# Hybrid decoder step on one core: another listed order of the instructions on all five engines

## Chip, cores and metric

The kernel runs on one core of a Trainium2 chip. The metric is device time in microseconds. The engines are PE (TensorE; PEld is its weight loads), DVE (VectorE), ACT (ScalarE), POOL (GpSimd) and SP (SyncE, which issues the transfers here). Each engine works through its own instructions strictly in the order in which they stand, and waits where an instruction needs something that another engine or a transfer has not delivered.

## What is computed

One step of a one-layer decoder, for a prompt of 2048 tokens and 8 samples of 8 new tokens each, model width 1024, all in f32:

```python
h = rmsnorm(x, norm_w)
z = h @ w_in
q, k, v, qb, kb, vb, g_lr, gate_a, gate_b = jnp.split(z, split_points(), axis=-1)
...
q = rope(rmsnorm(heads(q, H_A), q_norm_w), pos)
k = rope(rmsnorm(heads(k, H_A), k_norm_w), pos)
o_a = attend(q, k, v)
log_a = jax.nn.log_sigmoid((g_lr @ w_gate_up + b_gate).astype(jnp.float32)) / GATE_TAU
o_b, s_fin = gla_chunked(heads(qb, H_B) * (DK_B ** -0.5), heads(kb, H_B), heads(vb, H_B),
                         heads(log_a, H_B), s0)
o_b = rmsnorm(o_b, gla_norm_w)
mixed = jnp.concatenate([o_a.reshape(B, L, D_A) * jax.nn.silu(gate_a.astype(jnp.float32)),
                         o_b.reshape(B, L, D_B) * jax.nn.silu(gate_b.astype(jnp.float32))], axis=-1)
y = x + mixed.astype(x.dtype) @ w_out
```

`attend` mixes three dilated windows, (128,1), (512,4) and (2048,16), over 8 heads of 64. For the samples it reads a cache of 2048 keys and values. `gla_chunked` is gated linear attention, 4 heads with keys of 64 and values of 128. The outputs are y, the new keys and values and the final states.

## The kernel before

**Stages.** Weights and activations are split into a high and a low f16 part, so a projection of 128 rows by 512 columns is 24 matmuls of 128x128 weights on 512 columns (8 blocks of depth, 3 products): `project`, line 1632, tiles `acc_v`, `acc_q`, `acc_k`, `acc_qkb`, `acc_g`, `acc_vb`, `acc_gb`. The stages overlap:

- up to about 30 us: rows of x are scaled, turned and split (`prep_first`), and the weights w_v are scaled;
- to about 400 us: the v, q and k projections, and from 148 us on among them the window attention (`attend`): scores `s` (line 902), exp `p` on DVE and ACT (910, 913), transposes `t` (920), their split `pt` (877 to 887) and products `O` (935);
- to about 740 us: the rest of that attention, the last dilated branch from 534 us on, beside the qkb, g and vb projections (574 to 819 us for g and vb) with their silu (`so_g`, lines 1171 to 1185, on DVE and ACT);
- to about 1070 us: gated linear attention (`gla_core`, `gla_prompt`), first the samples', from 819 us on beside the gb projection, from 981 us on beside the output projection `Y` (`finish`, line 1991);
- to the end: `Y`, the turning of its inputs (`tm`, line 1956), and the samples' attention (`sample_pair`).

**Narrow matmuls.** Most matmuls use all 128x128 of TensorE's array. Some name a smaller part of it, a tile of the array. Their output then fills only some partitions, for instance 64 or 32, and others may fill the rest:

- `sc_e` (line 746, scores of gated linear attention): 128x64 tiles on 64 columns of f32, eight to a level, in turn for partitions 0 to 63 and 64 to 127;
- `U` (line 1790, the state's update): 128x64 tiles on 128 columns, four to a chunk of 128 tokens, two for each half;
- `R` (line 2182, the samples' scores) and `OS` (line 2248, their values): 128x32 tiles, in fours, one for each quarter of the partitions;
- `O_s` (1857), `U_s` (1890), `u_e` (681), `ptg_smp` (669) and the lower halves of the samples' projections (line 1323), fewer of each.

In the source the four OS of a step stand together:

```python
                for x, (u, bb) in enumerate(QUADS):
                    PE.matmul(
                        OS[32 * x : 32 * x + 32, 0:256], ps(x),
                        vs_[bb][:, 256 * u : 256 * u + 256],
                        start=(i == 0), stop=(i == 13),
                    )
```

**ScalarE's tables.** The first statement, `ACT.preload_act_table_set("natural_log_exp_and_others")` at line 566, loads the one set of tables that serves ln, exp, square and copy alike. Where ACT meets a function that the loaded set lacks, the build puts a load ahead of it.

**What sets the order.** The source is written in an order made by generators that `weave` takes turns with. That order is not the one that runs: at the end `in_order` (line 546) reads, for each engine, a list of numbers from `ORDER`, the places of the engine's instructions as written, and chains the instructions in the listed order:

```python
    for e, runs in ORDER.items():
        ends = [[int(n) for n in r.split("-")] for r in runs.split()]
        order = [traced[e][n] for r in ends for n in range(r[0], r[-1] + 1)]
        assert len(order) == len(traced[e])
        for a, b in zip(order, order[1:]):
            tc.add_manual_dep(b, a.name, info, reason="listed order")
```

The waits between engines follow from the data and the buffers, whatever the list. 8019 numbers stand for PE, 2014 for DVE, 1731 for ACT, 474 for POOL and 1055 for SP.

Of the kernel before, what the change touches and what calls it, by code (L numbers as in the profile page):

```python
# [53 lines left out]
        "6-8 0 2-3 1 10 4-5 9 11-25 74 90-91 75 92-93 76-77 94-99 78-79 100-111 80-89 112-113 26-33 42-46 "  # L54
        "34-41 47-65 116-129 140-146 66 147-160 67-68 161 114 69-71 162 72-73 163 130-131 115 132-139 "
        "164-212 214-218 213 219-281 286 282-283 287 284 288 285 289-295 310-312 296-298 313 299-304 314 "
        "305-309 315-387 390-392 397 426 398-399 427 404-405 428 406 433 409 434 410 435 411 440 416 441 "
        "417 442 418 447 421 448-449 422 454-455 423 456 461-463 468-470 475-477 484-486 491-493 500-502 "
        "509-511 516-518 525-527 532-534 539 546-548 557-559 564-566 571 540 572-573 541 582-584 587-589 "
        "592-594 601-603 610-612 615-617 622-624 629-634 639-641 658 646 659 647 660 665-667 670-671 648 "  # L60
        "672 651 675 652 676-677 653 682-684 689-691 694 706-708 711 695 712-713 696 716 699 717 700 718 "
        "701 723-725 730-732 735-737 742 754-756 761-763 743 766 744 767 749 768 750 771 751 772-773 "
        "778-780 785-787 792-794 799-801 806-808 811-813 818-820 827-829 836-838 843-845 852-854 861-863 "
        "866-868 873-875 884-886 891-893 898-900 388-389 393-396 400-401 909-911 916-918 407-408 412 402 "
        "413 419 403 420 424 414 425 415 921-923 930-931 429 932 939-941 944-945 443-446 946 436-439 430 "
        "457-458 431-432 464-465 459-460 466-467 450-453 489-490 494-495 471 953-955 962 514-515 519-520 "
        "963 482-483 487-488 507-508 512-513 472-474 478-481 496-499 503-506 521 964 967 542-545 968-969 "
        "567-570 972-973 535-538 560-563 522-524 528-531 549 974 574 979-980 984 550-555 575-581 597 556 "
        "590-591 595-596 985-986 613-614 618 991 598-600 604-607 585-586 992 608 993 609 619 998-999 620 "
        "1000 1003 635-638 1004 654-657 1005 981 621 625-626 642 627 643 628 644-645 649-650 1010-1012 "  # L70
        "661 1015-1017 662-664 680 1022 673-674 678-679 681 685-686 1023 668 692-693 669 697-698 1024 687 "
        "1027 688 1028-1029 702 1034-1036 703-705 714-715 721 719-720 709 1037 733-734 738-739 722 "
        "726-727 1038 710 1039 728 1040 729 752-753 757 740 758 774-777 1041 741 745-748 1042-1043 759 "
        "1044-1045 769 1046-1047 760 764-765 770 1048-1049 1056-1057 781 795-798 1058 816-817 788 782-784 "
        "802 789 821 790-791 1059 822 1060 809-810 1061 814-815 1062 823 1063-1067 803-805 824-826 "
        "830-833 1068-1071 841-842 846 834-835 847 869-870 848 871-872 839-840 859 849-851 855-856 860 "
        "876 857-858 864-865 887 877-883 888 894-897 901 889-890 919-920 924-925 902-908 926 912-915 "
        "927-928 937 942-943 947-948 929 933-936 965-966 970-971 938 960 949 961 950-952 975 956-958 "
        "1078-1080 1083 987-988 976-977 989-990 1084-1085 1006-1009 959 982 1086-1087 983 1088 1093-1095 "
        "1100-1101 1025-1026 1030-1031 1102 1105-1107 1124-1126 1131-1132 1112 1133 1054-1055 1113 1138 "  # L80
        "1114 1139 1119 1140 1120 1145 1121 1146-1147 1152-1154 1161-1163 1170-1172 1175-1177 1001 "
        "1182-1184 1193-1195 1200-1201 1072-1073 1202 1207-1209 1218-1219 1248-1250 1255 1220 1256 978 "
        "994 1225 995-997 1257 1226 1264 1227 1265 1230 1266 1231 1273 1232 1274 1239 1275 1240-1241 "
        "1280-1282 1285-1287 1296-1297 1310-1312 1321 1298 1322 1303 1323 1304 1328 1305 1329-1330 1002 "
        "1335-1337 1342-1344 1351 1013-1014 1018-1019 1352 1032 1353 1020 1052-1053 1358 1376-1378 "
        "1383-1385 1359 1392 1033 1050-1051 1360 1021 1393 1367 1394 1368 1399 1369 1400-1401 1089-1091 "
        "1406 1108-1110 1081 1074 1092 1111 1082 1075-1077 1407 1096-1098 1438 1408 1099 1439 1413 "
        "1103-1104 1440 1414 1449 1415 1450 1424 1122 1451 1425 1454 1426 1143-1144 1148-1149 1455 1431 "
        "1123 1129 1150 1127 1456 1432 1130 1151 1128 1115-1117 1134 1155 1118 1433 1461 1135 1157 1156 "
        "1462 1136-1137 1141-1142 1463 1466 1158-1160 1164-1167 1185 1467-1468 1477 1502-1503 1186 1504 "  # L90
        "1187 1478 1188 1509 1479 1510 1189-1190 1168 1196-1197 1191 1198 1192 1199 1169 1484 1178 1203 "
        "1173 1511 1179 1204 1174 1485 1180 1205 1181 1514 1206 1486 1515 1491 1516 1492 1523 1493 "
        "1524-1525 1532 1210 1533-1534 1539 1228 1253 1540 1221 1246-1247 1211 1251 1212-1213 1252 "
        "1214-1217 1235-1236 1222 1237-1238 1223 1242-1243 1229 1254 1224 1233 1258 1541 1564 1234 1259 "
        "1565 1548 1244 1566 1245 1549 1569 1550 1570 1557 1571 1558 1260 1580 1559 1581 1271 1261-1262 "
        "1272 1263 1267 1278 1299-1300 1306 1268-1269 1276 1279 1307 1277 1283 1301 1270 1288 1302 1582 "
        "1289-1290 1308 1291-1292 1284 1293 1309 1294 1587 1295 1588 1626 1589 1627 1594 1628 1595 1635 "
        "1596 1636 1605 1637 1606 1642 1324 1349-1350 1354-1355 1607 1313 1643 1314-1315 1325 1316 1612 "
        "1317 1326 1644 1318-1319 1327 1613 1320 1338 1651 1339-1340 1614 1341 1331 1356 1345 1652 1346 "
        "1332 1357 1347 1619 1348 1333 1361 1620 1653 1660 1621 1334 1362 1661-1662 1667 1363-1366 1668 "  # L100
        "1370-1373 1669 1388-1391 1381 1676 1374-1375 1409 1395 1379 1396 1382 1410 1380 1402-1403 "
        "1397-1398 1386 1411 1404-1405 1677 1387 1412 1678 1683-1685 1416 1690-1691 1417-1418 1692 "
        "1419-1420 1697-1699 1708-1709 1427-1430 1421-1423 1710 1452-1453 1434 1459-1460 1464 1457-1458 "
        "1441 1435-1437 1465 1442-1448 1715 1754-1756 1763 1487-1488 1764-1765 1770 1469-1472 1771 "
        "1473-1475 1489 1476 1772 1480-1481 1494 1490 1512-1513 1482 1517-1518 1483 1505 1495-1496 1506 "
        "1779 1497-1498 1507 1499-1500 1508 1716 1780 1501 1717 1781 1722 1788 1519 1723 1789 1520-1521 "
        "1724 1522 1790 1793-1795 1800 1530-1531 1733-1734 1555 1535 1556 1735 1560-1561 1738 1526-1528 "
        "1536 1529 1739 1801 1537 1740 1802 1562 1538 1563 1542 1745 1543 1572 1811 1567-1568 1544-1545 "
        "1746 1812 1546-1547 1551 1747 1552 1573-1579 1597-1602 1813 1553-1554 1603-1604 1590-1592 "
        "1583-1584 1615-1616 1585-1586 1617 1593 1618 1818-1820 1825-1827 1608-1609 1640 1610 1641 "  # L110
        "1645-1646 1611 1622 1665-1666 1670-1671 1836-1838 1623-1625 1629-1631 1633-1634 1632 1843-1844 "
        "1647 1845 1638-1639 1848-1849 1878 1658-1659 1850 1663-1664 1879 1857 1880 1672 1858 1885 1859 "
        "1648-1650 1654-1657 1886 1866 1887 1867 1894 1868 1895 1873 1896 1874 1901 1875 1902 1673-1675 "
        "1679-1682 1700-1707 1903 1906 1693-1696 1686-1687 1907-1908 1688-1689 1917 1711-1713 1718 1714 "
        "1719-1721 1918-1919 1924-1925 1743-1744 1748-1749 1926 1931 1725 1932 1736-1737 1741-1742 1933 "
        "1768-1769 1773-1774 1726-1731 1761-1762 1732 1766-1767 1750 1942-1943 1775 1944 1776 1949 "
        "1777-1778 1782-1783 1950 1784 1951 1956-1958 1963 1796-1799 1786-1787 1964 1821-1824 1791-1792 "
        "1965 1972-1974 1979-1981 1988 1846-1847 1851-1852 1989-1990 1871-1872 1997-1998 1751-1752 "
        "2004-2006 2013-2015 2020-2022 2027-2028 1999 2029 2034 1753 1757 2035 1758-1760 2036 2045-2046 "
# [2286 lines left out]
```

## Time and profile before

| | |
|---|---|
| median of 3 runs | 1242.07 us (1238.44 to 1246.38) |
| the profiled execution, span | 1241.8 us |
| mean granted clock of TensorE | 0.998 |
| PE busy | 1187.4 us, 96% |
| DVE, ACT, POOL busy | 942.0, 817.9, 544.5 us |
| HBM | 208 GB/s over the span |

The profiled execution's own time is given by its span, from the first to the last instruction. In the rows, `PE L1790 MATMUL U<-vb,kdt_e 128*64 128x128 f32 x2` reads: engine, line of the source, operation, tile written, tiles read, weights (rows * columns), moving operand, count. A matmul of f32 that is no transpose stands as two records. Matmuls are pipelined, so the length of one record is longer than the distance to the next start; for the pace of PE one reads distances between starts.

### The profile page before, as it was taken

Reading aid. Unit: us, or ns where it says so; the run is one execution under the profiler, and the core shown is the slowest. Engines: PE = TensorE matmul, PEld = TensorE weight load, DVE = VectorE, ACT = ScalarE, POOL = GpSimd, SP = SyncE. Lnnn points to the kernel's source line nnn. Section 1 sums busy time; section 2 is a strip of 40 time slices with the busy share of each in tenths; the row PEclk is TensorE's granted clock in tenths of the full one; section 3 lists DMA queues with packets and bytes.
Section 4 is the critical chain, followed back from the end, with each engine's and each line's share of the span. In section 5 each row is a group of like instructions: output and inputs, shape, how many; then the busy total and the mean of one; then the engine's idle time right before and its main releaser. Section 6 shows DMA issues by size and latency. Waiting matters only on the chain.

```text
span 1241.8 us, 26175 instructions
## 1 busy us (share of the span) xinstructions
PE 1187.4 (96%) x8942; PEld 715.1 (58%) x8942; DVE 942.0 (76%) x2457; ACT 817.9 (66%) x2184; POOL 544.5 (44%) x478
## 2 busy tenths in 40 slices
PE   4999999999999999999999899999999999999998
PEld 2444465566666656666776575645555665555543
DVE  7987779888988957668776666688999999833562
ACT  6654698789789978968865553468879864421220
POOL 0064433565647335552444456655634444501220
PEclk9999999999999999999999999999999999999999
DMA  8668956977866798789999887865773477899971
GB/s 279 224 197 229 224 153 154 228 220 201 192 187 170 201 249 288 227 233 266 267 244 245 229 245 215 233 198 185 222 258 94 154 243 243 274 349 372 399 278 50
DMA packets 235831, 283.07 MB, mean 228 GB/s; under 512 B 116193, under 2 KB 146866, under 8 KB 232626
## 3 DMA queue, kind: packets, MB, share of 16 engines
q1 hardware_dynamic: 235698, 281.40, 76.4%
q8 instruction: 71, 1.16, 0.4%
q14 instruction: 62, 0.51, 0.1%
HBM read 183.02 MB, written 75.24 MB: 208 GB/s over the span
## 4 chain that ended last, share of the span: by engine, by line
PE 52%; DVE 15%; ACT 12%; DMA 10%; issue 5%; POOL 4%; SPq 2%; POOLq 0%; DVEq 0%; ACTq 0%
PE Y L1991 9%; PE acc_k L1632 6%; PE acc_v L1632 5%; PE acc_q L1632 5%; PE acc_gb L1632 4%; ACT p L913 3%; PE t L920 3%; PE s L902 3%; PE O L935 3%; DMA k<-in_cache_k_win 2%; DMA qb<-q_d 2%; POOL pr L1487 2%; PE acc_qkb L1632 2%; PE OS L2248 2%; DVE p L910 2%
## 5 line engine op out<-in xcount | busy, mean ns | idle before, releaser
L1487 POOL TENSOR_TENSOR pr<-k,qb 128x512 f32<-128x512 f32 x128 | 167.9, 1312 | 172.4 <-DVE sck L1488 75.6
L1632 PEld LDWEIGHTS <-hr 128*128 128x128 f16 x1824 | 172.8, 98 | 111.7 <-issue 11.8
L913 ACT ACTIVATE p<-p,o 128x256 f32<-128x256 f32 (+1 forms) x384 | 172.9, 455 | 27.6 <-DVE o L910 20.8
L1632 PEld LDWEIGHTS <-hl 128*128 128x128 f16 x1248 | 119.4, 98 | 119.6 <-issue 7.4
L1991 PE MATMUL Y<-w_o,mh 128*128 128x512 f16 x768 | 180.3, 379 | 0.1
L887 POOL TENSOR_TENSOR pt<-p,pt 128x512 f16<-128x512 f32 (+1 forms) x80 | 91.4, 1142 | 123.5 <-ACT pt L884 96.2
L935 PE MATMUL O<-v,pt 128*128 128x128 f16 x1200 | 135.8, 220 | 8.4 <-DVE pt L880 2.8
L1488 DVE TENSOR_REDUCE sck<-pr 128x8 f32<-128x512 f32 x128 | 87.0, 679 | 53.9 <-POOL pr L1487 53.8
L920 PE MATMUL t<-ident,p 128*128 128x128 f32 x600 | 121.4, 280 | 5.5 <-ACT p L913 3.7
L935 PEld LDWEIGHTS <-pt 128*128 128x128 f16 x1200 | 94.9, 99 | 40.5 <-POOL pt L887 5.4
L1991 PEld LDWEIGHTS <-mh 128*128 128x128 f16 x768 | 72.3, 98 | 78.7 <-issue 4.9
L1632 PE MATMUL acc_g<-w_g,hr 128*128 128x272 f16 (+1 forms) x768 | 109.2, 276 | 2.0 <-ACT vbs L1274 1.5
L1632 PE MATMUL acc_v<-w_v,hl 128*128 128x512 f16 x384 | 110.0, 383 | 1.1 <-DVE vp L1287 0.8
L1632 PE MATMUL acc_q<-w_q,hl 128*128 128x512 f16 x384 | 109.6, 379 | 0.8 <-DVE vp L1287 0.6
L1632 PE MATMUL acc_k<-w_k,hl 128*128 128x512 f16 x384 | 108.4, 379 | 1.6 <-DVE vp L1287 1.5
L1632 PE MATMUL acc_vb<-w_vb,hr 128*128 128x512 f16 x384 | 95.2, 379 | 1.4 <-DVE so_g L1174 1.4
L910 DVE CUSTOM_DVE_ANT_0 p<-s,m3w,scl_s 128x128 f32<-128x128 f32 (+1 forms) x256 | 87.1, 394 | 9.7 <-DMA o_d<-o 4.6
L1632 PE MATMUL acc_gb<-w_gb,hr 128*128 128x512 f16 x384 | 94.1, 380 | 0.1
L920 PEld LDWEIGHTS t<-ident,p 128*128 128x128 f32 x600 | 75.4, 141 | 28.9 <-ACT p L913 14.1
L902 PE MATMUL s<-kk,qq 128*128 128x256 f16 (+1 forms) x512 | 85.1, 264 | 5.9 <-DMA kk<-kp_d 3.1
L1632 PE MATMUL acc_qkb<-w_qkb,hr 128*128 128x512 f16 x288 | 81.5, 379 | 0.1
L2033 POOL TENSOR_TENSOR oc<-oc 128x512 f32<-128x512 f32 x32 | 40.1, 1270 | 86.0 <-DVE oc L2026 67.7
(543 smaller groups left out, 2485.4 us busy)
## 6 DMA issues: line engine op xcount, KB each, us to landing
k<-in_cache_k_win SPq DMA_DIRECT2D x104, 256.0 KB
sv_b<-in_cache_v_win SPq DMA_DIRECT2D x24, 1024.0 KB
hr<-h_d SPq DMA_DIRECT2D x44, 512.0 KB
qb<-q_d SPq DMA_DIRECT2D x64, 256.0 KB
oc<-o_d SPq DMA_DIRECT2D x48, 264.0 KB
o_d<-o SPq DMA_DIRECT2D x64, 132.0 KB
x<-in_x_prompt SPq DMA_DIRECT2D x16, 512.0 KB
h_d<-hl SPq DMA_DIRECT2D x16, 512.0 KB
```

What stands on the lines that cost most here:

```text
L887: POOL.tensor_tensor(l, f, h, ALU.subtract)
L902: PE.matmul(s_ps[:, i * w : (i + 1) * w], q, k, start=(n == 0), stop=(n == len(prods) - 1),)
L910: DVE.tensor_tensor_reduce(s[:, sl], s_ps[:, sl], mask, neg, BIG, ALU.add, ALU.min, nmf(i))
L913: ACT.activation(s[:, sl], s[:, sl], AF.Exp, bias=nmf(i), scale=-1.0, accum_out=denf(i))
L920: PE.transpose(p_ps[:, i * P : (i + 1) * P], t["s"][:, i * P : (i + 1) * P], ident[:])
L935: PE.matmul(o_, t["pt"][:, c, (i * nb + b) * P : (i * nb + b + 1) * P], vf(i, b), start=(n == 0), stop=(n == 2 * nb - 1),)
L1487: POOL.tensor_tensor(pr[:], kt, qt, ALU.mult)
L1488: DVE.tensor_reduce(out, pr[:].rearrange("p (u k d) -> p u k d", u=2, k=4), AX.X, ALU.add)
L1632: PE.matmul(z, a_[:, k, :], w[:, p_, k, cols], start=(k == 0 and i == 0), stop=(k == KT - 1 and i == 2),)
L1991: PE.matmul(Y[:], a_[:, k, :], w_[:, part, k, :512], start=(i == 0), stop=(i == len(prods) - 1),)
L2033: eng.tensor_tensor(o_[g], o_[g], w[:, g].unsqueeze(2).to_broadcast([P, NH, HD]), ALU.mult)
L2248: PE.matmul(OS[32 * x : 32 * x + 32, 0:256], ps(x), vs_[bb][:, 256 * u : 256 * u + 256], start=(i == 0), stop=(i == 13),)
```

## The change

`ORDER` holds other lists, for all five engines; it grows from 494 to 676 lines, so every line of the source below it has a number higher by 182. Nothing else differs. Of the PE list, 592 of 8019 numbers keep their place; a number moves by 14 places in the mean and by 216 at most. On DVE the mean is 4.2, on ACT 2.9, on POOL 1.2 and on SP 4.9. The beginnings of two of the lists:

```diff
     "PE": (
-        "6-8 0 2-3 1 10 4-5 9 11-25 74 90-91 75 92-93 76-77 94-99 78-79 100-111 80-89 112-113 26-33 42-46 "
...
+        "6 0 2 10 3 11 4-5 1 12-13 7 14-15 8 18-19 16-17 20-23 9 24 74 25 90-93 75-76 94-95 77 "
...
     "Activation": (
-        "0 2-7 1 8-12 18 15 19 13 20-21 14 22-23 16 24 17 25-28 32 29-30 33-35 31 44-46 36-42 47-49 43 "
...
+        "2-3 5 4 6 1 7 9-10 8 12 11 18 15 13 0 19-20 14 21 16-17 23 25 22 26-27 24 28-29 32-35 "
...
```

On PE, in the last stage, where OS of the first pair of samples begins (Y is the output projection, tm and tk are transposes, R the scores of the next pair). Before:

```order
L1956 LDWEIGHTS mt_15055
L1956 MATMUL tm_0_15324<-ident_83,mt_15055 128x128
L2248 MATMUL OS_15118<-vs_t,Pn_15111 32x256 x4
L2248 MATMUL OS_15118<-sv_0_w,P_0_15109 32x256
L2248 MATMUL OS_15118<-sv_1_w,P_0_15109 32x256
```

and so on, 56 OS without anything between. Now:

```order
L2430 MATMUL OS_15118<-sv_0_b_15131,P2x 32x256
L2138 LDWEIGHTS mt_15055
L2138 MATMUL tm_1_15334<-ident_83,mt_15055 128x128
L2173 LDWEIGHTS mh_14971
L2173 MATMUL Y_0_15020<-w_o_13021,mh_14971 128x512
L2138 LDWEIGHTS mt_15055
L2138 MATMUL tm_0_15324<-ident_83,mt_15055 128x128
L2430 MATMUL OS_15118<-sv_1_b_15133,P2x 32x256
L2364 MATMUL R_15304<-ksT,qx 32x64
L2430 MATMUL OS_15118<-sv_0_b_15131,P2x 32x256
```

The OS of one group of four are parted by matmuls of the full array.

On PE, beside the gb projection, one level of the scores of gated linear attention. Before:

```order
L1804 MATMUL O_11987<-vb_11980,full 128x128
L1632 LDWEIGHTS hr_13309
L1632 MATMUL acc_gb_13556<-w_gb,hr_13309 128x512
L746 MATMUL sc_e_16_12346<-qbd_9604,kq_e_12117 64x64 x8
L1790 MATMUL U_11982<-vb_11980,kdt_e_11949 64x128 x2
```

Now:

```order
L1814 LDWEIGHTS hr_13388
L1814 MATMUL acc_gb_13669<-w_gb,hr_13388 128x512
L928 MATMUL sc_e_16_12346<-qbd_9604,kq_e_12117 64x64
L1814 LDWEIGHTS hr_13309
L1814 MATMUL acc_gb_13556<-w_gb,hr_13309 128x512
L928 MATMUL sc_e_16_12346<-qbd_9604,kq_e_12117 64x64 x7
```

The eight of the level are split into one and seven, with a wide matmul between, and the U that followed stand elsewhere.

On ACT, the first instructions (jk squares x, rr is ln and then exp, nwa a small absolute value). Before:

```order
L566 ACT_TABLE_LOAD
L975 ACTIVATE jk_s,ss_188<-x_s 64x1024
L629 ACTIVATE rr_xs<-rv_xs 64x1
L631 ACTIVATE rr_xs<-rr_xs 64x1
L975 ACTIVATE jk_205,ss_188<-x_160 128x1024
L629 ACTIVATE rr_x_208<-rv_x_207 128x1
L631 ACTIVATE rr_x_208<-rr_x_208,ln_h 128x1
L1511 ACTIVATE nwa<-nw 128x8
```

Now:

```order
L1157 ACT_TABLE_LOAD
L1157 ACTIVATE jk_s,ss_188<-x_s 64x1024
L811 ACT_TABLE_LOAD
L811 ACTIVATE rr_xs<-rv_xs 64x1
L1157 ACTIVATE jk_205,ss_188<-x_160 128x1024
L813 ACT_TABLE_LOAD
L813 ACTIVATE rr_xs<-rr_xs 64x1
L811 ACT_TABLE_LOAD
L811 ACTIVATE rr_x_208<-rv_x_207 128x1
L1693 ACTIVATE nwa<-nw 128x8
L813 ACT_TABLE_LOAD
L813 ACTIVATE rr_x_208<-rr_x_208,ln_h 128x1
```

The preload (line 566, now 748) has moved behind the first fifteen activations, and five loads that the build put in stand ahead of it.

1138 rows, old and new, of the table ORDER are left out of this document.

## The prediction

> **What bounds the kernel now.** I read the page first, then the stages, then the waits of TensorE, and last the rows of TensorE's own stream.
>
> ```profile
> PE 1187.4 (96%) x8942; PEld 715.1 (58%) x8942; DVE 942.0 (76%) x2457; ACT 817.9 (66%) x2184; POOL 544.5 (44%) x478
> PE 52%; DVE 15%; ACT 12%; DMA 10%; issue 5%; POOL 4%; SPq 2%; POOLq 0%; DVEq 0%; ACTq 0%
> ```
>
> The second line is the chain that ended last: half of it is TensorE. The stages:
>
> ```profile
> 0.00:31.00 31.00, 15.40 (x79) 7.75 (x80) 21.77 (x51) 20.45 (x35) 2.51 (x7) 1.00 0.85 279
> 31.00:190.00 159.00, 151.54 (x892) 78.80 (x889) 131.72 (x316) 104.34 (x267) 63.28 (x59) 1.00 0.71 201
> 190.00:420.00 230.00, 222.62 (x1671) 144.88 (x1672) 200.65 (x529) 197.58 (x560) 127.31 (x97) 1.00 0.75 192
> 420.00:640.00 220.00, 215.55 (x1718) 145.45 (x1717) 158.33 (x500) 174.37 (x533) 96.70 (x78) 0.99 0.92 256
> 640.00:785.00 145.00, 137.09 (x1041) 91.77 (x1039) 94.01 (x270) 74.58 (x245) 81.53 (x76) 1.00 0.85 226
> 785.00:930.00 145.00, 139.97 (x1056) 77.92 (x1055) 123.04 (x285) 108.26 (x259) 76.90 (x73) 1.00 0.74 229
> 930.00:1090.00 160.00, 157.83 (x1265) 94.70 (x1264) 147.28 (x358) 107.83 (x238) 75.74 (x74) 1.00 0.60 205
> 1090.00:1242.00 152.00, 147.36 (x1235) 73.88 (x1232) 65.23 (x152) 30.46 (x52) 20.51 (x18) 0.99 0.75 286
> ```
>
> A row gives the stretch, its length, busy time of PE, PEld, DVE, ACT and POOL, the granted clock (0.99 to 1.00 everywhere), DMA share and GB/s. TensorE is busy 1187.4 of 1241.8 us: 54.4 us are idle. Of these 12.1 us lie before its first matmul (the ptx row below). So a better order can win at most about 42 us by ending waits, and 4.4 of these are the tail behind the last matmul (the second row of Y below ends at 1237.4). The waits that are there now:
>
> ```profile
> PE ptx L1036 <- DVE wm_v L1118: 12.1, 1, 12.1
> PE t L920 <- ACT p L913: 3.7, 9, 0.6
> PE s L902 <- DMA kk<-kp_d: 3.1, 2, 2.4
> PE O L935 <- DVE pt L880: 2.8, 2, 2.6
> PE acc_vb L1632 <- DVE so_g L1174: 1.4, 1, 1.4
> ```
>
> They are many and small. But busy is not the same as filled: what matters on a bound TensorE is the distance from one start to the next. A wide matmul (128x128 weights) keeps this pace:
>
> ```profile
> 1159.61 10.47 PE Y L1991 x48
> 1226.96 10.48 PE Y L1991 x48
> ```
>
> That is 0.218 us for each of 48, so 0.216 between neighbours. Now the narrow ones, whose weights take only 32 or 64 columns of the array, or whose contraction takes only part of its rows. First one U alone, then four U together, then eight sc_e together, each between wide ones (start, length; f32 counts as two records):
>
> ```profile
> 896.73 0.81 PE L1632 MATMUL acc_gb<-w_gb,hr 128*128 128x512 f16 x3
> 897.47 0.43 PE L1790 MATMUL U<-vb,kdt_e 128*64 128x128 f32 x2
> 897.84 0.82 PE L1632 MATMUL acc_gb<-w_gb,hr 128*128 128x512 f16 x3
> ...
> 1062.90 0.81 PE L1991 MATMUL Y<-w_o,mh 128*128 128x512 f16 x3
> 1063.64 0.66 PE L1790 MATMUL U<-vb,kdt_e 128*64 128x128 f32 x8
> 1064.23 0.60 PE L1991 MATMUL Y<-w_o,mh 128*128 128x512 f16 x2
> ...
> 920.09 1.03 PE L1632 MATMUL acc_gb<-w_gb,hr 128*128 128x512 f16 x4
> 921.04 0.69 PE L746 MATMUL sc_e<-qbd,kq_e 128*64 128x64 f32 x16
> 921.66 0.61 PE L1632 MATMUL acc_gb<-w_gb,hr 128*128 128x512 f16 x2
> ```
>
> One U: from 896.73 to 897.84 are 1.11 us, less three wide ones (0.65) leaves 0.46. Four U: 1.33 less 0.65 leaves 0.68. So four cost hardly more than one. With f a fee for going from wide to narrow and back, and p the time of one record: one U is f + 2p = 0.46, four U are f + 4p = 0.68, if two that write different halves of the partitions run side by side. That gives p = 0.11 and **f = 0.24 us**. The eight sc_e check it: 1.57 less 0.86 leaves 0.71, and with half as many columns p = 0.054, so 8p = 0.43 and f = 0.28. The same fee is paid by each of several narrow ones that alternate with wide ones:
>
> ```profile
> 751.05 0.27 PE L669 MATMUL ptg_smp<-ident,zqk_smp 64*128 64x64 f32 x1
> 751.26 0.29 PE L1632 MATMUL acc_g<-w_g,hr 128*128 128x272 f16 x1
> 751.48 0.27 PE L669 MATMUL ptg_smp<-ident,zqk_smp 64*128 64x64 f32 x1
> ```
>
> One round is 0.43 us here. The wide one is worth 272/512 of 0.216, that is 0.115, and the narrow one one record of 64 columns, 0.054: 0.26 is fee. And the biggest narrow block, 32 columns wide, four to a row of the array:
>
> ```profile
> 1098.76 6.32 PE OS L2248 x112
> ```
>
> 112 records are 56 matmuls. A record moves 256 columns of f32, twice p of U, 0.216. One after the other they would take 24 us. They take 6.3: four run side by side, 28 steps of 0.216 being 6.05, and a fee. Only narrow transposes that write at the left edge go free: T with 128*64 weights starts at 1097.79 and the next wide one at 1097.90, 0.11 us later.
>
> ```profile
> 1097.79 0.27 PE L2228 MATMUL T<-ident,spr 128*64 128x128 f32 x1
> 1097.90 0.81 PE L1991 MATMUL Y<-w_o,mh 128*128 128x512 f16 x3
> ```
>
> **The change, part by part.** No instruction of arithmetic and no transfer is added. What moves on TensorE is how finely kinds are mixed. I counted in the listed order of PE unbroken runs of narrow matmuls, without those free transposes: 127 before, 431 now, with the same 937 matmuls in them. (Families that touch make one run here; below they are counted apart.)
>
> First term, the fee: 304 more runs by 0.24 are **+73.0 us**. The ends are 67 (0.22, since the starts are rounded to 0.01 us) and 85 (0.28, the sc_e rows; OS and the alternating rows lie between with 0.27 and 0.26). I take 0.24, from the pair of U rows, since most new runs are one or two matmuls long, like the lone U.
>
> Second term, what no longer runs side by side. For each run, matmuls that follow each other and write different strips count as one step, otherwise each takes its own two records. Summed over the runs of one family at a time:
>
> - OS (224 matmuls): 7 runs now become 102, 60 of them a single matmul. Steps worth 24.1 us become 49.5: a lone OS takes 2 x 0.216 where it took a quarter of that.
> - sc_e of width 64 (390): 55 runs become 186, 105 single; 21.3 becomes 27.7.
> - R (64): 5 become 43; 2.6 becomes 6.8. U (64): 24 become 52; 8.0 becomes 11.8.
> - lower halves of the sample projections (80): 16 become 43; 7.8 becomes 10.7. O_s (16): 3.9 becomes 6.0.
>
> The differences are 25.4, 6.4, 4.2, 3.8, 2.9 and 2.1: **+44.8 us**. The lower end is 43.8, if neighbours of different families pair up too. The upper one is 55: OS and sc_e have 18 and 39 runs of two, 8 and 15 of three; if none of these paired they would take 20 us more, and I allow half of it.
>
> Both terms lie on TensorE's path and behind no other work: in the last three stages, where most of these runs are, TensorE idles 12 of 457 us (145.0 less 140.0, 160.0 less 157.8, 152.0 less 147.4), so nothing is there to take 118 us.
>
> Third term, waits that end. From 31 to 785 us TensorE idles 27 us (the four rows of stages), from 785 on about 7 besides its tail. The new order spreads attention more evenly: of the handoffs from exp to the transposes t, those with under 1 us of TensorE work between the scores and their transpose fall from 13 to 3. On the other side, the cover for silu's release of the accumulators (so_g, 38 handoffs before, 42 now) shrinks from a median of 3.9 to 1.3 us of TensorE work. I take 12 us off in attention and 8 behind it, where the longer narrow work itself covers what other engines owe: **-20 us**. The ends are -34, all of it, and +20, if thinner covers cost more than they save.
>
> Fourth term, ScalarE's tables. The instruction that loads the one table with both ln and exp stood first; it now stands behind 15 activations, and five more loads appear. The row of one:
>
> ```profile
> 0.73 1.28 ACT L566 ACT_TABLE_LOAD   x1 [0.73 <-PEq L2389]
> 13.28 0.21 ACT L1511 ACTIVATE nwa<-nw 128x8 f32<-128x8 f32 x1 [4.20 <-DMA nw<-in_norm_w]
> 18.91 0.72 ACT L1155 ACTIVATE w_v<-wr_v,ns_v 128x512 f16<-128x512 f32 x1 [0.95 <-DVE ns_v L1146]
> ```
>
> Loads before 13.28 fall into time in which ScalarE waits for x and nw (4.20 us there alone). Two come behind it, ahead of the scaling of the first x tile and among the w_v copies that feed the first matmuls: 2 x 1.28, **+2.6 us**; 0 if the nw transfer comes sooner, 6.4 if all five show.
>
> The Trainium skill, "ScalarE: Activation LUTs", section "What ACT_TABLE_LOAD costs", counts 2.66 us for a switch, a drain of 1.38 being part of it. By it this term would be 5.3 instead of 2.6 and the sum 1344.9. The row shows the load alone, so its drain is not refuted here.
>
> The Trainium skill, "TensorEngine Tiling (Array Packing)", section "Key Properties", says that changing the tiling mode drains TensorE and that different tiles work in parallel. This speaks against the change; it gives no price. Counting every change of mode by that rule (320 before, 933 now) at half a fee each would give 613 x 0.12, so 73.6 in place of 73.0; the free T row does not bear out that every change drains.
>
> The sum stands against the profiled execution: 1241.8 + 73.0 + 44.8 - 20 + 2.6 = **1342.2 us**. That execution is 0.3 us from the median of 1242.07, so nothing is added for it.
>
> **The rivals.** (A) Faster: narrow matmuls slip into idle time of TensorE and cost nothing there, and the waits end. It decides if the two TensorE terms together stay below the idle 38 us that lie neither at the start nor in the tail of 4: 1241.8 - 38 + 2.6 = 1206. For it speaks that the page shows waits all over attention. Against it speaks the round of 0.43 us at 751, in which a mixed order without any wait pays the fee each time.
>
> (B) The fee hides, the lost pairing does not. A wait for a semaphore may stand where the entry would, and the array drains meanwhile: 1241.8 + 44.8 - 20 + 2.6 = 1269. For it: a run that begins with a wait pays no entry. Against it: with 96% busy there are too few waits for 431 runs.
>
> (C) Slower still: thin covers become the bound in the projection stage. If each of the 42 so_g handoffs waited 1.4 us like the one in the rows above, that is 59 us: 1342 + 59 = 1401. Against it: the fee lengthens the cover as well.
>
> That the change does not do what it says is out: the built programs show the mixed order on PE.
>
> **How the numbers follow.** My sum has a chance of 0.76, B 0.10, C 0.08, A 0.04, and 0.02 goes to a mixture that ends within 1%. The predicted time is 1342.2. All low ends together are 1241.8 + 67 + 43.8 - 34 + 0 = 1319, all high ends 1241.8 + 85 + 55 + 20 + 6.4 = 1408. All at once is unlikely on the high side, so the range stops at 1390, short of C; below it goes on half the way to B: 1295 to 1390. Within 1% is about what a measurement of this kernel can't tell from no change. Faster by over 1% is A, 0.04; within 1% 0.02; slower by over 1% is my sum, B and C, 0.94.
>
> **What would show it.** If I am right, the profile after shows TensorE still busy at 95% or more over a longer span, its growth nearly all behind 785 us of the old program; OS steps of one matmul taking about 0.67 us between wide ones (0.24 + 2 x 0.216), U alone 0.46, sc_e alone 0.35; fewer and shorter waits of t for p; five more table loads in the first 25 us. The forecast is wrong if lone narrow matmuls take 0.1 to 0.2 us between wide ones, or if the idle time of TensorE grows by more than the fee does.

## The result, and the profile after

| | before | changed |
|---|---|---|
| median | 1240.41 us (1238.44 to 1246.38, 4 runs) | 1356.31 us (1350.32 to 1358.49, 4 runs) |
| profiled execution, span | 1241.8 us | 1354.2 us |
| PE busy, and idle | 1187.4, 54.4 us | 1296.1, 58.1 us |

The ratio is 1.093 (95% interval 1.089 to 1.097): the new order is slower. The forecast was 1342.2, with a range from 1295 to 1390. The first lines of the changed kernel's page:

```profile
PE 1296.1 (96%) x8942; PEld 736.6 (54%) x8942; DVE 918.8 (68%) x2457; ACT 827.9 (61%) x2189; POOL 539.6 (40%) x478
PE 75%; DMA 8%; DVE 7%; ACT 6%; issue 2%; POOL 1%; SPq 1%; DVEq 0%; ACTq 0%; POOLq 0%
```

TensorE has the same 8942 records, is busy for 109 us more, and is three quarters of the chain that ended last instead of half. Of the other engines only ACT grew, by 10 us (PEld, TensorE's own weight loads, by 21.5). The stages of the changed kernel, cut at the same times as before (stretch, length, busy time of PE, PEld, DVE, ACT, POOL):

```profile
0.00:31.00 31.00, 11.54 (x50) 5.32 (x50) 16.44 (x45) 24.93 (x38) 2.52 (x7) 1.00 0.69 231
31.00:785.00 754.00, 719.88 (x5241) 456.71 (x5242) 567.86 (x1604) 553.02 (x1599) 359.58 (x300) 1.00 0.81 217
785.00:1242.00 457.00, 456.87 (x3055) 232.02 (x3059) 290.83 (x719) 233.79 (x530) 162.76 (x160) 1.00 0.61 202
1242.00:1354.00 112.00, 107.85 (x605) 42.54 (x594) 43.64 (x90) 16.14 (x24) 14.79 (x12) 1.00 0.50 182
```

Up to 785 us the two kernels get through nearly the same number of matmul records (5291 here, 5401 before: the sums of the counts of PE). Behind it TensorE never rests (456.87 of 457 us) and yet needs 112 us longer. This is the picture of a busy engine whose time goes into something else than columns. What it goes into can be seen in single rows; beside the gb projection, and in the last stage:

```profile
1004.91 0.39 PE L1814 MATMUL acc_gb<-w_gb,hr 128*128 128x512 f16 x1
1005.23 0.33 PE L928 MATMUL sc_e<-qbd,kq_e 128*64 128x64 f32 x2
1005.49 0.39 PE L1814 MATMUL acc_gb<-w_gb,hr 128*128 128x512 f16 x1
1005.81 0.43 PE L1972 MATMUL U<-vb,kdt_e 128*64 128x128 f32 x2
1006.17 1.25 PE L1814 MATMUL acc_gb<-w_gb,hr 128*128 128x512 f16 x5
...
1203.10 0.39 PE L2173 MATMUL Y<-w_o,mh 128*128 128x512 f16 x1
1203.42 0.62 PE L2430 MATMUL OS<-sv_w,P 128*32 128x256 f32 x2
1203.97 0.39 PE L2173 MATMUL Y<-w_o,mh 128*128 128x512 f16 x1
```

From one wide start to the next, less 0.216 for the wide one, a lone sc_e takes 0.36 us, a lone U 0.46 and a lone OS 0.65. Over all lone ones between wide ones the medians are 0.355 (87 cases), 0.459 (19) and 0.645 (45).

The weight loads in the same trace show where this time lies. Between two wide matmuls the second one's load starts while the first runs: at 1006.18 us for a matmul that starts at 1006.40. At the lone OS each load starts only together with its own matmul, at 1203.42 for OS and at 1203.97 for the Y behind it. From the start of Y to that of OS are 0.32 us, and from the second record of OS to the next Y 0.31, where the pace is 0.216: about 0.1 us of the fee at each change of kind. The transpose T that goes free in the kernel before has its load ahead of it (1097.69, matmul 1097.79).

**The ledger of narrow runs.** It is made from the starts of all matmuls in the two traces. For each unbroken run of narrow matmuls it takes the distance from the wide start ahead of the run to the wide start behind it, less the pace of the wide one. From this the steps of the run are taken off (matmuls that write different strips, quarters or halves of the partitions, side by side count once). What is left is the fee and, where a run begins with a wait, the wait.

| | before | changed | difference |
|---|---|---|---|
| runs with both neighbours in the trace | 126 | 430 | +304 |
| time in and around them | 134.2 | 246.1 | +111.9 |
| of it steps | 89.1 | 133.0 | +43.9 |
| of it left over, runs without a wait | 31.1 (106 runs) | 111.0 (427 runs) | |
| of it left over, runs with a wait | 13.9 (20 runs) | 2.1 (3 runs) | |

What is left over is 0.260 us for a run without a wait (median 0.247). With 0.25 us of fee inside each run that waits, the fees are 36.1 and 111.8, **+75.7 us**, and the waits 8.9 and 1.4, -7.5 us. All 112 us of the narrow runs' growth but 6 lie behind 785 us. The same reckoning between neighbouring wide matmuls gives what these wait for other engines, behind the first matmul: up to 31 us 0.7 before and 4.4 now, from there to 785 us 37.2 and 40.1, behind it 6.6 and 0.2. These sizes depend by one or two us on what is taken as the pace; their signs do not. The stages agree: from 31 to 785 us TensorE idles 34.1 us, where it idled 27.2.

Then the waits. TensorE's own in the changed kernel (times in us in total, how many, longest):

```profile
PE ptx L1218 <- DMA ident<-in_c_ident: 12.7, 1, 12.7
PE s L1084 <- DVE o L1092: 7.2, 11, 1.7
PE acc_qkb L1814 <- ACT zq L1434: 2.4, 1, 2.4
PE acc_vb_s L1502 <- ACT w_vb L1337: 2.1, 2, 1.5
PE acc_vb L1814 <- DVE so_g L1356: 2.0, 2, 1.7
PE acc_g L1814 <- DVE so_g L1356: 1.9, 2, 1.3
PE t L1102 <- ACT p L1095: 1.8, 4, 0.8
```

Waits of t for p fell from 3.7 us (9) to 1.8 (4), and the 3.1 us that s waited for a transfer (kk) are gone. Waits of s for DVE rose from 2.7 us (3) to 7.2 (11). Summed over the waits listed between 31 and 785 us, attention's own (s, t and O) are 18.3 us before and 17.3 now; those of the projections (acc, the samples' among them) rise from 5.8 to 13.8.

### The profile page after: what moved, and what is told of

Its sections match the earlier page's. It is cut to its first block, busy times and chain, and to the rows that moved or that the text cites. A ratio compares the mean times of both kernels' runs of the same rounds, so it can differ in the third digit from the quotient of the medians.

```text
span 1354.2 us, 26101 instructions
## 1 busy us (share of the span) xinstructions
PE 1296.1 (96%) x8942; PEld 736.6 (54%) x8942; DVE 918.8 (68%) x2457; ACT 827.9 (61%) x2189; POOL 539.6 (40%) x478
## 4 chain that ended last, share of the span: by engine, by line
PE 75%; DMA 8%; DVE 7%; ACT 6%; issue 2%; POOL 1%; SPq 1%; DVEq 0%; ACTq 0%; POOLq 0%
PE Y L2173 13%; PE acc_gb L1814 7%; PE acc_g L1814 4%; PE acc_v L1814 4%; PE OS L2430 4%; PE acc_k L1814 4%; PE acc_vb L1814 4%; PE acc_qkb L1814 4%; PE sc_e L928 4%; PE acc_q L1814 4%; PE s L1084 3%; PE O L1117 3%; PE t L1102 3%; DMA o_d<-o 3%; PE tm L2138 1%
## 5 line engine op out<-in xcount | busy, mean ns | idle before, releaser
L1814 PEld LDWEIGHTS <-hr 128*128 128x128 f16 x1824 | 165.5, 98 | 107.0 <-issue 27.1
L2173 PE MATMUL Y<-w_o,mh 128*128 128x512 f16 x768 | 204.6, 381 | 0.1
L1095 ACT ACTIVATE p<-p,o 128x256 f32<-128x256 f32 (+1 forms) x384 | 173.5, 454 | 37.9 <-DVE o L1092 36.1
L1117 PE MATMUL O<-v,pt 128*128 128x128 f16 x1200 | 187.5, 219 | 7.5 <-DVE pt L1062 3.1
L1102 PE MATMUL t<-ident,p 128*128 128x128 f32 x600 | 141.9, 277 | 3.1 <-ACT p L1095 1.8
L1814 PE MATMUL acc_g<-w_g,hr 128*128 128x272 f16 (+1 forms) x768 | 137.1, 277 | 2.8 <-DVE so_g L1356 1.9
L1117 PEld LDWEIGHTS <-pt 128*128 128x128 f16 x1200 | 109.5, 98 | 55.2 <-issue 7.6
L1084 PE MATMUL s<-kk,qq 128*128 128x256 f16 (+1 forms) x512 | 113.6, 264 | 6.0 <-DVE o L1092 5.8
L1814 PE MATMUL acc_vb<-w_vb,hr 128*128 128x512 f16 x384 | 116.5, 382 | 2.0 <-DVE so_g L1356 2.0
L2173 PEld LDWEIGHTS <-mh 128*128 128x128 f16 x768 | 66.9, 98 | 80.6 <-issue 27.6
L1814 PE MATMUL acc_gb<-w_gb,hr 128*128 128x512 f16 x384 | 105.8, 382 | 0.0
```

What stands on the lines that cost most here:

```text
L1084: PE.matmul(s_ps[:, i * w : (i + 1) * w], q, k, start=(n == 0), stop=(n == len(prods) - 1),)
L1095: ACT.activation(s[:, sl], s[:, sl], AF.Exp, bias=nmf(i), scale=-1.0, accum_out=denf(i))
L1102: PE.transpose(p_ps[:, i * P : (i + 1) * P], t["s"][:, i * P : (i + 1) * P], ident[:])
L1117: PE.matmul(o_, t["pt"][:, c, (i * nb + b) * P : (i * nb + b + 1) * P], vf(i, b), start=(n == 0), stop=(n == 2 * nb - 1),)
L1814: PE.matmul(z, a_[:, k, :], w[:, p_, k, cols], start=(k == 0 and i == 0), stop=(k == KT - 1 and i == 2),)
L2173: PE.matmul(Y[:], a_[:, k, :], w_[:, part, k, :512], start=(i == 0), stop=(i == len(prods) - 1),)
```

## The experiments

No kernel was run with one engine's list taken from the one kernel and the others' from the other: engines would then wait in a circle, each for something that stands later on another. This is argued, not tried. What can be done is to move matmuls inside TensorE's list, to change the order in the source inside a run, and to use one order for all engines up to a point and the other behind it. Medians of before, run beside each group, were 1239.9 to 1241.2 us.

### Narrow matmuls of the changed kernel together again, in pairs and fours

```diff
+def together(written, order, sizes):
+    key, members = narrow_groups(written, sizes)
+    out = []
+    for i in order:
+        out += members.pop(key[i.name], []) if i.name in key else [i]
+    return out
...
+        if e == "PE":
+            order = together(traced[e], order, {"sc_e": 2, "U_": 2, "OS_": 4, "R_": 4, "O_s": 2, "half": 2})
```

`narrow_groups` numbers the narrow matmuls of each output tile as written and puts so many neighbours into one group.

> The changed kernel with one edit in TensorE's list: matmuls of the same tile that write different strips (two sc_e, two U, four OS, four R, two O_s, two lower halves) stand next to each other again, at the place of the first of them. Runs of narrow matmuls fall from 431 to 306, and all of the lost side-by-side work comes back (133.0 us of steps to 89.3). Theory (fee and pairing are two separate prices): 1356.3 - 43.9 - 125 x 0.25 = 1281 us, 1270 to 1295. Rival P (there is only one price, a flat 0.37 us for each additional run, which is 112 us over 304 runs): 1356.3 - 46 = 1310. Rival W (the loss is a matter of waits, from the order of the other four engines, which stays as changed): 1340 or more.

Measured: 1286.73 us (1285.71 to 1287.79), ratio 1.037 (1.034 to 1.040). The theory of two prices said 1281 (1270 to 1295), the single price 1310. In the trace the steps are back at 89.2 us, and 299 runs without a wait leave 0.272 us each. So 70 of the 116 us come back from TensorE's list alone, with the four other engines' order as changed.

### The same in whole blocks

The same edit with `{"sc_e": 8, "U_": 2, "OS_": 16, "R_": 8, "O_s": 2, "half": 8}`.

> The changed kernel, with larger blocks gathered in TensorE's list: eight sc_e, sixteen OS, eight R, eight lower halves, two U and two O_s at the place of the first. 176 runs in place of 431, steps back at 89.3 us; the lists of DVE, ACT, POOL and SP and the order of the wide matmuls stay as changed. Theory: 1356.3 - 43.9 - 255 x 0.25 = 1249 us, 1238 to 1263, so within 1% or so of the kernel before. Rival P: 1356.3 - 255 x 0.37 = 1262, and the step from the paired version is 130 x 0.37 = 48 us where the theory says 32. Rival W: 1320 or more, since the other engines' order is untouched.

Measured: 1269.68 us (1266.42 to 1274.79), ratio 1.024 (1.020 to 1.028). This is 20 us more than the theory's 1249 and above its range. The number is near the rival's single price, 1262, but the trace does not bear that out: 155 runs without a wait leave 45.1 us where the paired version had 81.3 over 299. Runs with a wait leave 16.3 us (20 runs; 2.9 over 6 there). With 0.25 us of fee inside each of these, fees fell by 33 us (theory 32, rival 48), and what came instead are waits: 10 us more at narrow runs, and 5.6 more at wide ones. These make 17 us less, as the medians say; the profiled executions differ by 11, but that of the block version is its slowest run, at a granted clock of 0.992 (0.996 in the paired one). A block that is gathered at the place of its first member needs all its inputs at that time. One row shows the largest:

```profile
PE acc_v_s L1530 <- DVE w_v L1363: 3.7, 1, 3.7
```

This is a block of eight lower halves that stands for the last part of its weights.

### Blocks, with that wait mended and the table load in front

The lower halves are gathered in pairs (`"half": 2`), and

```diff
+        if e == "Activation":
+            order.remove(traced[e][0])
+            order.insert(0, traced[e][0])
```

> The version with blocks gathered, with two things mended that its profile shows as waits: the lower halves of the sample projections are gathered in pairs in place of eights (the block of eight stood waiting 4.3 and 1.5 us for its weights), and ScalarE's table load is back in the first place. 196 runs in place of 176, steps 89.3 us as there. Theory: 1269.7 - 5.8 (that wait) - 3.9 (three table loads that show in the front) + 20 x 0.25 = 1265 us, 1258 to 1270. If the version with blocks was slow for another reason than these waits: 1270 or more.

Measured: 1267.03 us (1262.29 to 1268.37), ratio 1.020 (1.016 to 1.023), within the theory's range. In the trace the row of 3.7 us is gone, and TensorE is busy 15.28 us up to 31 us, where it was busy 11.02. But the gain in time over the version with blocks (2.7 us, 4.7 forecast) is within the two ranges, and other waits grew (t for p from 2.8 to 3.7 us, acc_qkb for zq from 2.5 to 3.0). So the two waits are removed, and what they were worth in time is not shown.

### Side by side taken away, no run more

The kernel before, with the order in the source changed inside the runs:

```diff
-            for c in range(nch):
-                for p in range(2):
-                    o = (c * 2 + p) * 64
-                    for k0 in range(0, C, 64):
+            for k0 in range(0, C, 64):
+                for c in range(nch):
+                    for p in range(2):
+                        o = (c * 2 + p) * 64
...
                 for x, (u, bb) in enumerate(QUADS):
-                    PE.matmul(
+                    for n, (ps, vs_) in enumerate(pieces_):
+                        PE.matmul(
```

> The kernel before, with side-by-side work taken away and not one run more: inside each run the matmuls are written strip by strip (sc_e: all that write the lower 64 partitions, then all that write the upper; OS: the whole sum of one strip of 32 columns, then the next), so that neighbours write the same strip. 127 runs as before. Steps by the rule that only neighbours on different strips share a step: sc_e +15.5, OS +44.3 us. Theory: 1240.4 + 60 = 1300 us, 1285 to 1312. Rival P (price per run only): 1240. A third way, that the array looks further ahead than the next matmul and still pairs them: also 1240 to 1260.

Measured: 1277.29 us (1276.68 to 1279.37), ratio 1.030 (1.027 to 1.033). So lost pairing has a price with not one run more, which the single price per run denies. But it is 37 us, not 60, and the time lies below the forecast range. The rows of the strip-by-strip kernel show where the rule was too strict:

```profile
929.33 1.47 PE L1632 MATMUL acc_gb<-w_gb,hr 128*128 128x512 f16 x6
930.73 0.97 PE L746 MATMUL sc_e<-qbd,kq_e 128*64 128x64 f32 x16
931.63 0.61 PE L1632 MATMUL acc_gb<-w_gb,hr 128*128 128x512 f16 x2
...
1106.31 0.64 PE L2249 MATMUL OS<-vs_t,Pn 64*32 64x256 f32 x8
1106.88 0.64 PE L2249 MATMUL OS<-sv_w,P 128*32 128x256 f32 x8
1107.33 3.92 PE L2249 MATMUL OS<-sv_b,P2x 128*32 128x256 f32 x29
1110.88 0.40 PE L2249 MATMUL OS<-sv_b,P3x 128*32 128x256 f32 x1
...
1111.77 7.28 PE L2249 MATMUL OS<-sv_b,P3x 128*32 128x256 f32 x60
1118.98 0.39 PE L1991 MATMUL Y<-w_o,mh 128*128 128x512 f16 x1
```

A block of OS takes 12.67 us (1106.31 to 1118.98) where it took 6.32, and eight sc_e take 1.00 (2.30 less six wide ones) where they took 0.71. Four blocks and 48 levels make 25.4 and 13.9, together 39 us. One strip after the other would have taken 44.3 more for OS. From 1107.33 to 1110.88, 29 records of P2x start in 3.55 us, 0.122 each and not 0.216: about two strips are at work at a time, though neighbours in the list write the same strip.

### Two of one strip, then two of the next

The same edit for OS alone, with the four steps of a piece taken two at a time (`for j in range(0, n, 2)`).

> The kernel before with OS alone written in twos: two matmuls of one strip of 32 columns, then two of the next, and so on; sc_e as before, no run more. If a strip holds two waiting matmuls while the next one goes to another strip (as the trace of the strip-by-strip version looks: two strips at work at a time when four in a row belong to each): little or nothing is lost, 1240 to 1248 us. By the rule that only neighbours on different strips share a step: +23.6, 1264 us.

Measured: 1240.68 us (1236.51 to 1245.73), ratio 1.000 (0.998 to 1.002). The block of OS:

```profile
1096.50 0.64 PE L2249 MATMUL OS<-vs_t,Pn 64*32 64x256 f32 x8
1097.07 0.64 PE L2249 MATMUL OS<-sv_w,P 128*32 128x256 f32 x8
1097.52 1.97 PE L2249 MATMUL OS<-sv_b,P2x 128*32 128x256 f32 x32
1099.25 3.71 PE L2249 MATMUL OS<-sv_b,P3x 128*32 128x256 f32 x64
1102.89 0.39 PE L1991 MATMUL Y<-w_o,mh 128*128 128x512 f16 x1
```

It takes 6.39 us, as in turn (6.32). So a second matmul of the same strip does not hold up the one behind it that goes to another strip; four in a row do.

### Runs cut up, no pair parted

The kernel before, with one wide matmul that followed a run put behind each pair or four of it (of `acc_`, `Y_` and `tm_`):

```diff
+        for j, g in enumerate(groups):
+            out += g + order[m : w][j : j + 1]
```

> The kernel before, with runs cut up and no pair parted: behind each pair of sc_e or U, each four of OS or R of a run one of the wide matmuls that followed the run is put between, so that 127 runs become 285, while matmuls that ran side by side still do (steps 89.3 us, unchanged). Theory: the fee alone, 158 x 0.25 = 39, so 1240.4 + 39 = 1280 us, 1270 to 1290. Rival P: 1240.4 + 158 x 0.37 = 1298. If the fee hides in TensorE's own overlap: 1240 to 1250.

Measured: 1281.34 us (1279.33 to 1283.33), ratio 1.032 (1.029 to 1.036). That is +41.4 us for 158 runs, 0.262 each, with steps of 89.6 us in the trace. The fee is there by itself, and has the size that the pair of U rows gave. One piece of it:

```profile
1126.18 0.23 PE L2004 MATMUL tm<-ident,mt 128*128 128x128 f16 x1
1126.34 0.64 PE L2296 MATMUL OS<-sv_b,P2x 128*32 128x256 f32 x8
1126.91 0.23 PE L2004 MATMUL tm<-ident,mt 128*128 128x128 f16 x1
```

From tm to tm are 0.73 us; less 0.054 for tm (128 columns), four OS with their fee cost 0.68, and a lone one cost 0.65 above.

### The new order up to 785 us, then the old, and the other way round

Both tables stand in the file. `CUT` holds, for each engine, how many instructions of the first kernel had begun at 785 us of its profile; those run in its order, all the rest in the other's:

```diff
-        order = [traced[e][n] for r in ends for n in range(r[0], r[-1] + 1)]
+        listed = [n for r in ends for n in range(r[0], r[-1] + 1)][: CUT[e]]
+        early = set(listed)
+        ends = [[int(n) for n in r.split("-")] for r in LATER[e].split()]
+        listed += [n for r in ends for n in range(r[0], r[-1] + 1) if n not in early]
+        order = [traced[e][n] for n in listed]
```

> The new order of all five engines for what starts before 785 us in the changed kernel's profile (attention and all that runs beside it: 5273 of 8019 matmuls), then the old order for all the rest. Counted on TensorE: 160 runs in place of the old 127, and steps of 92.0 in place of 89.3 us, so narrow work should add 33 x 0.25 + 2.7 = 11 us. What is left is the prediction's third and fourth term by themselves. As predicted (12 us of attention's waits end, tables 2.6): 1240.4 + 11 - 12 + 2.6 = 1242 us. What the two profiles say instead (TensorE's idle time up to 785 us is 27.2 before and 34.1 in the changed one, first matmul 0.6 later, some 2 for the tables): 1240.4 + 11 + 7 + 2.6 = 1261 us, 1253 to 1268.

Measured: 1260.53 us (1258.18 to 1264.56), ratio 1.016 (1.014 to 1.019). The forecast by the prediction's own terms was 1242, that by the two profiles 1261.

```profile
0.00:31.00 31.00, 11.86 (x47) 5.34 (x48) 15.87 (x44) 24.25 (x37) 2.51 (x7) 1.00 0.68 228
31.00:785.00 754.00, 722.76 (x5247) 458.14 (x5246) 572.66 (x1605) 553.57 (x1600) 357.06 (x300) 0.99 0.80 217
```

TensorE is busy 3.5 us less in the front (15.40 before) and idles 31.2 us up to 785, against 27.2. So up to 785 us the new order ends no waits in sum.

> The counterpart: the old order of all five engines for what starts before 785 us in the profile of before, then the new order for all the rest. 391 runs and steps of 128.4 us on TensorE, no late table loads. Theory (fee and lost pairing, nothing else): 1240.4 + 264 x 0.25 + 39.1 = 1346 us, less up to 8 where the longer narrow work covers other engines' waits: 1335 to 1348. Rival (the loss comes from the new order's attention part): under 1300.

Measured: 1337.31 us (1334.88 to 1341.52), ratio 1.078 (1.076 to 1.081), +96 us and within the forecast range. The two halves together (+19 and +96) make up the whole of +116. Nearly all of the loss comes from the part with the narrow matmuls, as the prediction had it.

### The table load in front

The changed kernel with the load of ScalarE's table first in its list (the diff above) and nothing else.

> The changed kernel with ScalarE's load of the table with ln and exp back in the first place of its list; nothing else. The five further loads should be gone. Prediction's fourth term (two loads show, 1.28 us each): 1356.3 - 2.6 = 1354 us; if a switch costs 2.66 us, as the Trainium skill has it (ScalarE: Activation LUTs, What ACT_TABLE_LOAD costs), 1351. So small a difference is read from when the first accumulations start in the profile (acc_v waits for w_v at 24.4 us in the changed kernel), not from the median.

Measured: 1348.64 us (2 runs: 1348.27 and 1349.02), ratio 1.087 (1.085 to 1.089). The median is 7.7 us lower, but not taken beside the changed kernel, and its profile has a granted clock of 1.000 (0.997 in the changed kernel's), so the front is read instead. ScalarE in the changed kernel:

```profile
8.90 1.28 ACT L813 ACT_TABLE_LOAD   x1
10.20 0.20 ACT L813 ACTIVATE rr_xs<-rr_xs 64x1 f32<-64x1 f32 x1
10.42 1.28 ACT L811 ACT_TABLE_LOAD   x1
11.71 0.20 ACT L811 ACTIVATE rr_x<-rv_x 128x1 f32<-128x1 f32 x1
11.82 0.19 ACT L1693 ACTIVATE nwa<-nw 128x8 f32<-128x8 f32 x1
12.03 1.28 ACT L813 ACT_TABLE_LOAD   x1
13.33 0.30 ACT L813 ACTIVATE rr_x<-rr_x,ln_h 128x1 f32<-128x1 f32 x1
14.70 1.15 ACT L1204 ACTIVATE x<-x,rs 128x1024 f32<-128x1024 f32 x1 [1.08 <-DVE rs L816]
...
22.36 1.28 ACT L748 ACT_TABLE_LOAD   x1
23.66 1.33 ACT L1337 ACTIVATE w_v<-wr_v,ns_v 128x512 f16<-128x512 f32 x2
```

and with the load in front:

```profile
9.94 0.29 ACT L816 ACTIVATE rr_x<-rr_x,ln_h 128x1 f32<-128x1 f32 x1
12.11 1.15 ACT L1207 ACTIVATE x<-x,rs 128x1024 f32<-128x1024 f32 x1 [1.88 <-DVE rs L819]
```

x is scaled 2.6 us sooner. The load at 22.36 is gone as well, and the transposes th that TensorE starts at 30.00 us in the changed kernel start at 26.11: 3.9 us, what three loads of 1.28 make. The stage up to 31 us agrees: TensorE is busy 15.70 us in it, 4.2 more than in the changed kernel.

### The fee turned to use

The kernel before, with runs merged: where at most eight wide matmuls of `acc_`, `Y_` or `tm_` stand between two narrow runs, the first run is moved behind them.

```diff
+        if (a, w, c) == ("narrow", "wide", "narrow") and len(y) <= most:
+            runs[n - 1 : n + 2] = [["wide", y], ["narrow", x + z]]
```

> The kernel before, with TensorE's list improved by the theory's rule: where at most eight wide matmuls of the projections or of tm stand between two runs of narrow ones, the first run is moved behind them, so that the two become one. 103 runs in place of 127, steps unchanged. Theory: 24 x 0.25 = 6 us less, 1234 us, if nothing that waits for the first run is on the path; if the moved runs make other engines late, 1240 or more.

Measured: 1259.16 us (1256.77 to 1259.78), ratio 1.015 (1.013 to 1.017): 18 us slower, where 6 faster was expected. In the ledger the fees of runs without a wait fall from 31.1 to 24.5 us, as they should, and what is left over at runs with a wait rises from 13.9 to 35.5. Its waits:

```profile
PE sc_e L773 <- POOL kq_e L740: 8.6, 10, 0.9
PE sc_e L773 <- ACT qbd L732: 5.0, 6, 1.6
```

The two in the kernel before:

```profile
PE sc_e L746 <- ACT qbd L705: 1.6, 5, 0.4
PE sc_e L746 <- POOL kq_e L713: 0.4, 1, 0.4
```

They rise by 11.6 us, about half of the 21.6. What links them to the move is argued: a level's scores that come up to 1.7 us later (eight wide ones) free the buffers of kq_e and qbd later, and so the inputs of a later level come later. This was not tried by itself. None of the versions that were run beats the kernel before.

## Why the prediction was right, and where it was not

**The views** led to the right place: a TensorE that is busy 96% of the time, read by distances between starts.

**First term, the fee** (+73.0 forecast): +75.7 in the ledger. The cut version has it alone, 0.262 us for each further run. The lone rows are those that were forecast: OS 0.645 us (0.67), U 0.459 (0.46), sc_e 0.355 (0.35). The Trainium skill, "TensorEngine Tiling (Array Packing)", section "Key Properties", says that changing the tiling mode drains TensorE. The runs agree, but for the free T, and give a price, which the page does not. Whether it is a drain, or a weight load that starts late, they do not tell apart.

**Second term, side by side** (+44.8): +43.9. That the strip-by-strip version loses 37 us with no run more shows that it is a price of its own. Its rule, that only neighbours on different strips share a step, is too strict for long runs of one strip. Here it did no harm, since the new order parts the matmuls by wide ones and so leaves few such runs.

**Third term, waits that end** (-20): this step failed by half. Waits at narrow runs fell by 7.5 us. Those at wide matmuls behind 785 us fell from 6.6 to 0.2, so that the part behind attention gave more than the 8 allowed. But the part up to 785 us gave nothing of its 12: waits at wide matmuls went from 37.2 to 40.1 us there. The handoff that was counted, exp to the transposes, did get better (3.7 to 1.8 us). Two others that were not taken off the 12 got worse by more. One is the projections: their waits rose by 8.0 us. Of this the accumulators that wait for so_g, whose thinner cover the prediction named as a risk, are 2.3 (1.6 to 3.9); acc_qkb and acc_vb_s in the rows above are 4.5. Why these two come late was not looked into. The other is the scores that wait for DVE (2.7 to 7.2 us). DVE's own waits show what may be late there, before and in the changed kernel:

```profile
DVE p L910 <- DMA o_d<-o: 5.6, 6, 1.5
```

```profile
DVE p L1092 <- DMA o_d<-o: 19.8, 15, 3.6
```

Lines 910 and 1092 are DVE's masking of the scores, which also writes each row's extreme into an o buffer. It waits for the transfer that empties that buffer, and the next scores wait for DVE. The version with the new order up to 785 us shows both again: there DVE waits 25.0 us (18) for the transfer, and the scores 6.1 us (11) for DVE. That the one causes the other is argued only; no run gave o another buffer. That version also shows the outcome without most of the narrow matmuls: no gain.

**Fourth term, tables** (+2.6, two loads): 3.9, three loads. Two of them lie ahead of x, which is scaled 2.6 us sooner without them, and one among the w_v copies (22.36); the prediction had one at each place. The norm weights came sooner than in the old order (nwa did not wait at 11.82), an end that the prediction named but expected to be of help; with that idle time gone, one more load lay open. The Trainium skill, "ScalarE: Activation LUTs", section "What ACT_TABLE_LOAD costs", counts a drain of 1.38 us beside a load of 1.28. This trace does not show it: the instruction ahead of the load at 12.03 ends at 12.01 (11.82 and 0.19), the load ends at 13.31, and the next activation begins at 13.33. By the page three loads would be 8.0 us; the runs say 3.9.

The four terms as measured are 75.7 + 43.9 - 11 + 3.9 = 112.5, against 112.4 between the two spans; the -11 are 7.5 and 6.4 less, and 2.9 more. The forecast of 1342.2 fell 12 us short of the profiled execution, and 9 of these are the third term. In that term a miss of 15 us up to 785 us is partly offset by about 6 us more than forecast behind it; that they offset each other is luck.

**The rivals.** A (the fee fits into idle time) and B (the fee hides behind waits) fall with the cut version, where 158 runs cost 0.262 us each. C (thin covers of so_g, 59 us) does not occur: the two rows above are 3.9 us.

## What to carry to other kernels

On a TensorE that is busy all the time, look at the distance between starts and count how often the stream goes from full to partial tiles and back: each such trip cost 0.25 us here, about one wide matmul of 512 columns, whatever it carried. An order that spreads small matmuls evenly among large ones looks better balanced, but it pays for each trip and loses the neighbour that would have run beside it. But to gather them blindly is no gain either: a block has to wait for its last input, and a run that is moved back by a microsecond may sit on a loop through other engines, so price the merge against the waits at that place.

## What was not expected of the hardware

- Matmuls of one strip queue behind each other without blocking the next strip for two in a row (block of OS 6.39 us against 6.32), not for four in a row (12.67).
- Four 128x32 matmuls of 256 columns cost 0.68 us between wide ones, one costs 0.65.
- Loads of ScalarE's tables follow and precede activations within 0.02 us; each costs its 1.28 us.
